# Interleaving the moving columns of a kernel's products, and reading the banks with a step of two

## The chip, the cores and the metric

One core of a Trainium2 chip runs the kernel. The metric is the device time of one execution in microseconds (us). Times and profile come from runs on the chip; the profile is that of one execution. In it PE is TensorE's matrix multiply, PEld its weight load, DVE is VectorE, ACT is ScalarE, POOL is GpSimd, SP issues DMAs.

## The reference

A transformer layer on 1024 rows of width 1024 in float32: a feed-forward block, a token mixer of two parallel groups (sparse attention with three branches, and a gated linear recurrence), a second feed-forward block, and a last norm.

```python
def swiglu(x, w_gu, w_down):
    gate, up = jnp.split(x @ w_gu, 2, axis=-1)
    return (jax.nn.silu(gate) * up) @ w_down

def hybrid_mixer(h, w_in, ...):
    parts = jnp.split(h @ w_in, IN_SPLITS, axis=-1)
    nq, k_c, v_c, k_s, v_s, k_w, v_w, gl, hq, hf, hi, hg = parts
    o_nsa = nsa_group(nq, k_c, v_c, k_s, v_s, k_w, v_w, gl, ...)
    o_hg = hgrn2_group(hq, hf, hi, hg, lower_bound, hg_norm)
    return jnp.concatenate([o_nsa, o_hg], axis=-1) @ w_out

h = h + 0.5 * swiglu(rms_norm(h, ffn1_norm[l]), ffn1_w_gu[l], ffn1_w_down[l])
h = h + hybrid_mixer(rms_norm(h, mix_norm[l]), w_in[l], ...)
h = h + 0.5 * swiglu(rms_norm(h, ffn2_norm[l]), ffn2_w_gu[l], ffn2_w_down[l])
return rms_norm(h, final_norm)
```

The hidden width of the feed-forward blocks is 2752.

## The kernel before

Each float32 operand of a large product is split into two parts that TensorE takes in its fast four-byte format: a rounded high part and the rest (`split`, line 152: ScalarE or GpSimd make the high part in line 157 or 155, VectorE the rest in line 159). A product is then three matrix multiplies into one accumulating bank: high by high, high by low, low by high (`mm3`, lines 161 to 165). A multiply loads a stationary operand of 128 columns and streams a moving operand of up to 512 columns past it. Its output fills a PSUM bank, 128 partitions by 512 float32, one bank column for each moving column.

The stages in order of time:

- The up projection of the first block (to about 470 us): the hidden width is cut into tiles `j` of 128 gate and 128 up columns. Most tiles are computed by `up_strassen` (line 645), a scheme with 7 block products in place of 8, of four `mm3` each. The moving operand is `xT`, 512 columns of the transposed input; the stationary one a piece `wp` of the weights. Three banks P, Q and T take the sums; VectorE adds them up (lines 659, 662, 671, 676, 680) and ScalarE copies one (line 656). `up_out` (line 519) applies the gate and writes the hidden tile `hk` out. `up_plain` and `up_last` do the first tiles and the last, narrow one.
- The down projection (`down`, line 685; to about 700 us): seven stages by the same scheme, 11 steps each; `products` (lines 715 to 717) streams 512 columns of the split weights `dw`. `copies` (line 702) and `add` (line 696) read the banks.
- The mixer (to about 1310 us): projections of queries, keys, values, gates (`gemm_fm`, `gemm_fm_steps` with moving `xT`, `gemm_tm_steps` in lines 780 to 782 with moving weights of 280 or 256 columns, `hgrn_values` and `wout`); the recurrence (`hgrn_unit`) with many small products; attention (`att_soft`, `att_pv`), where scores are products of lines 1219 and 1220, weights are transposed in line 1305, split in lines 1307 and 1308, and multiplied with the values in line 1296 with 512 moving columns (four heads by 128 queries).
- The second block, as the first (to the end).

In all of these the moving operand's columns are read from left to right, and what reads a bank (ScalarE and VectorE instructions) reads its columns from left to right as well. The banks come from pools of a few buffers, so a product into a reused bank waits until what reads it is done. Instructions of an engine run in the order in which they were issued; the pools and a few `late` and `ordered` sections set it.

Some moving reads are by nature of other shapes and aren't touched: scores (up to 512 columns of the keys), transposes, the recurrence's products of 32 to 128 columns, the compression's of 126. VectorE has reads with a step in line 931 (every second value of a tile, twice) and in line 1029 (through a view of `cr` in which neighbouring values lie 16 apart, 64 bytes).

Of the kernel before, what the change touches and what calls it, by code (L numbers as in the profile page):

```python
# [41 lines left out]

def offsets(spec):
    at, o = {}, 0
    for k, cols in spec.items():
        n = sum(b - a for a, b in cols)
        at[k] = o, n
        o += n * D
    return at


def tiled(w, spec):

# [19 lines left out]
class Net:  # L73
# [87 lines left out]
    def mm3(self, ps, wh, wl, xh, xl, first, last, skip=False):  # L161
        mm = self.nc.tensor.matmul
        mm(ps, wh, xh, start=first, stop=False, skip_group_check=skip)  # L163
        mm(ps, wh, xl, start=False, stop=False, skip_group_check=skip)  # L164
        mm(ps, wl, xh, start=False, stop=last, skip_group_check=skip)  # L165
# [353 lines left out]
    def up_out(self, H, j, half, g, u, R, n=128, dve=False):  # L519
# [51 lines left out]
    def up_plain(self, P, groups, js, ws, R, H):  # L571
# [3 lines left out]
        V = {}  # L575
        for ks in groups:
# [3 lines left out]
            for kts in ((0, 1), (2, 3)) if ks[0][2] else ((0,), (1,), (2, 3)):  # L580
                for j, e, o in ks:
# [4 lines left out]
                    if o == 0 and 3 in kts:  # L586
                        nc.scalar.activation(out=P[j, e], in_=V[j, e][:], func=AF.Copy)
            yield
        for j in js:
            self.up_out(H, j, 0, V[j, 0], V[j, 1], R, dve=True)  # L590
# [10 lines left out]
            for k, b in zip(ks, W):  # L601
                nc.vector.tensor_tensor(out=P[k], in0=b[:], in1=P[k], op=OP.add)
            self.up_out(H, j, 1, P[j, 0], P[j, 1], R, dve=True)
# [23 lines left out]
    def up_last(self, wpool, cpool, j, raw, R, H):  # L627
# [6 lines left out]
        nc.scalar.activation(out=p[:], in_=V[:], func=AF.Copy)  # L634
# [3 lines left out]
        u = ct("pu")  # L638
        nc.vector.tensor_copy(out=u[:64], in_=V[64:])
        self.up_out(H, j, 0, V, u, R, 64, True)  # L640
        nc.vector.tensor_tensor(out=p[:], in0=Wb[:], in1=p[:], op=OP.add)
        u = ct("pu")
        nc.vector.tensor_copy(out=u[:64], in_=p[64:])
        self.up_out(H, j, 1, p, u, R, 64, True)

    def up_strassen(self, cpool, j, w, nxt, R, H, sums):
# [7 lines left out]
        p, c12, c22 = ct("pp"), ct("pc"), ct("pd")  # L654
        self.up_mm(P[:], w[0], 0, True, True)
        nc.scalar.activation(out=p[:], in_=P[:], func=AF.Copy)
        step()
        self.up_mm(Q[:], w[1], 4, True, True)
        tt(out=c12[:], in0=Q[:], in1=p[:], op=OP.add)
        step()  # L660
        self.up_mm(T[:], w[2], 3, True, True)
        tt(out=c22[:], in0=T[:], in1=p[:], op=OP.add)
# [8 lines left out]
        tt(out=c22[:], in0=Q[:], in1=c22[:], op=OP.add)  # L671
# [4 lines left out]
        tt(out=c12[:], in0=T[:], in1=c12[:], op=OP.add)  # L676
# [3 lines left out]
        tt(out=p[:], in0=Q[:], in1=p[:], op=OP.add)  # L680
        step()
        self.up_out(H, j, 0, P, p, R, dve=True)
        return out

    def down(self, pool, pool2, name, H, h, scale, final, after=(), wide=None, tail=0):
# [7 lines left out]
        def add(half, t, c, src):  # L693
            tt = half * 4 + t
            hv = h[tt][:, c * 512:c * 512 + 512]
            nc.vector.scalar_tensor_tensor(out=hv, in0=src[:], scalar=scale(tt), in1=hv, op0=OP.mult, op1=OP.add)

        def copies(bs, tag):
            p = H["pool"] if tag == "hk" else pool2
            out = [p.tile([128, 512], F32, name=self.nm(tag), tag=tag, bufs=4) for _ in range(4)]  # L700
            for t in range(4):
                nc.scalar.activation(out=out[t][:], in_=bs[t][:], func=AF.Copy)
            return out
# [3 lines left out]
        for n, (an, bn) in enumerate(stages):  # L707
# [4 lines left out]
            def products(t, m, hh, hl, dh, dl):  # L712
                c = slice(t * 128, t * 128 + 128)
# [43 lines left out]
            for t in range(4):  # L757
                for a in left:
                    products(t, *a)
                if n in (1, 4, 5, 6):  # L760
                    half, c = {1: (1, 0), 4: (0, 0), 5: (0, 1), 6: (1, 1)}[n]
                    add(half, t, c, bs[t])
# [69 lines left out]
    def hgrn_proj(self, p, wp, x, hh, u, w=None):  # L832
# [3 lines left out]
        for half in range(2):  # L836
# [4 lines left out]
            nc.scalar.activation(out=q[:], in_=b[:], func=AF.Sigmoid)  # L841
            nc.vector.tensor_tensor(out=q[:], in0=b[:], in1=q[:], op=OP.mult)
# [4 lines left out]
            nc.scalar.activation(out=f[:], in_=b[:], func=AF.Sigmoid)  # L847
            nc.scalar.activation(out=k[:], in_=b[:], func=AF.Sigmoid, scale=-1.0)
# [4 lines left out]
    def hgrn_gate(self, wp, x, hh, u):  # L853
# [3 lines left out]
        for half in range(2):  # L857
# [3 lines left out]
            nc.scalar.activation(out=g[:], in_=b[:], func=AF.Sigmoid)  # L861
            nc.vector.tensor_tensor(out=g[:], in0=b[:], in1=g[:], op=OP.mult)

    def hgrn_values(self, p, wp, x, vs):
# [13 lines left out]
        for half in range(2):  # L878
            bs = [self.bank() for _ in range(4)]
            for kt in range(KT):  # L880
                for t, b in enumerate(bs):
                    c = slice(t * 128, t * 128 + 128)
                    self.mm3(b[:], x[0][kt // 2][half][:, kt % 2, c], x[1][kt // 2][half][:, kt % 2, c], *w[kt], kt == 0, kt == KT - 1)
                    if kt == KT - 1:
                        v = p.tile([128, 512], F32, name=self.nm("v"), tag="vg", bufs=8)
                        nc.scalar.activation(out=v[:], in_=b[:], func=AF.Copy)
# [103 lines left out]
    def compress_in(self, mop, w, x, raw):  # L990
# [3 lines left out]
        for half in range(2):  # L994
            for s, r in enumerate(raw):
                b = self.bank()
                self.gemm_fm(b[:], w, s * 128, 128, x, half)
                nc.scalar.activation(out=r[:, half * 512:half * 512 + 512], in_=b[:], func=AF.Copy)
# [92 lines left out]
    def att_proj_kv(self, p, wp, x):  # L1091
# [15 lines left out]
        for s in range(2):  # L1107
            for half in range(2):
# [3 lines left out]
                nc.scalar.activation(out=r[:], in_=b[:], func=AF.Copy)  # L1112
                self.kraw[s][half] = r

    def att_proj_q(self, p, wp, x, half, tag, tiles=range(4)):

        nc = self.nc
        for i in tiles:
# [8 lines left out]
            for e in range(2):  # L1127
# [3 lines left out]
                hi = t[g * 64:g * 64 + 64, :]  # L1131
                lo = t[64 - g * 64:128 - g * 64, :]
                src = b[e * 64:e * 64 + 64, :]
# [146 lines left out]
    def att_pv(self, p, g, qb, Ps, raw, M):  # L1280
# [12 lines left out]
        def pv(n):  # L1293
            i, c, w, v = blocks[n]
            for k, t in enumerate((th, tl)):
                mm(O[:], v, t[n][:w], start=n + k == 0, stop=n == last and k == 1)  # L1296
# [20 lines left out]
        nc.scalar.activation(out=tmp, in_=O[64:128].rearrange("p (h q) -> p h q", h=4), func=AF.Copy)  # L1317
        qc = slice((qb % 4) * 128, (qb % 4) * 128 + 128)
        r = p.tile([128, 4, 128], F32, name=self.nm("os"), tag="pt", bufs=5)[:, :2] if M else raw[:, :, qc]
        for e in range(2):  # L1320
            nc.vector.tensor_tensor(out=r[e * 64:e * 64 + 64], in0=O[0:64].rearrange("p (h q) -> p h q", h=4)[:, e::2, :],
                                    in1=tmp[:, e::2, :], op=OP.add)
# [4 lines left out]
    def wout(self, p, M, half, hspill):  # L1327
# [3 lines left out]
        for cq in range(4):  # L1331
            c = slice(cq * 256, cq * 256 + 256)
            w = self.wpages(cq, self.wq_tile)
            for tt in range(half * 4, half * 4 + 4):
# [6 lines left out]
                nc.vector.tensor_tensor(out=r[:], in0=b[:, :256], in1=r[:], op=OP.add)  # L1341
# [3 lines left out]
def body(ctx, tc, ins, out):  # L1345
# [355 lines left out]
    for c in range(2):  # L1701
# [35 lines left out]
        for i in range(4):  # L1737
            hv = h[i][:, c * 512:c * 512 + 512]
            nc.vector.tensor_tensor(out=hv, in0=bs[i][:], in1=hv, op=OP.add)
# [106 lines left out]
```

## Time and profile before

| what | value |
| --- | --- |
| time, median of 3 runs | 1974.97 us |
| lowest, highest | 1974.3, 1979.25 us |
| span of the profiled execution | 1975.0 us |
| mean granted TensorE clock | 0.999 |
| instructions | 31355 |
| matrix multiplies | 11054 |
| DMA | 304.31 MB, mean 154 GB/s |

The span is that from the first to the last instruction of the profiled execution; it is within 0.03 us of the median, so the time of that execution is its span as far as the runs can tell. A row of the groups gives line, engine, operation, output and input names, shapes and count, then the busy time in us and the mean ns of one, then the idle time before it and what ended it. A row of the timeline gives the start and the length in us. Matrix multiplies are pipelined: the recorded length of one reaches into the next, so that the distance of two starts, and not the length, is what a product costs in a row of products.

### The profile page before, as it was taken

How to read it: one execution, taken by the hardware profiler on the slowest of the kernel's cores; microseconds unless marked ns; L12 is line 12 of the kernel's file. 1: busy time of each engine (PE TensorE's matmuls, PEld its weight loads, DVE VectorE, ACT ScalarE, POOL GpSimd, SP SyncE). 2: the span in 40 equal slices, each digit the busy share in tenths (PEclk: the TensorE clock that was granted, in tenths of full speed). 3: DMA queues.
4: the chain of work that ended last, by engine and by line, in shares of the span. 5: the costliest groups of instructions: out<-in, count | busy, mean ns of one | idle time of the engine just before them, and what ended most of it. 6: DMA issues, size and time to landing. Idle time of an engine off the chain costs nothing.

```text
span 1975.0 us, 31355 instructions
## 1 busy us (share of the span) xinstructions
PE 1954.0 (99%) x11054; PEld 1617.0 (82%) x11054; DVE 1380.0 (70%) x2811; ACT 790.3 (40%) x1665; POOL 500.3 (25%) x612
## 2 busy tenths in 40 slices
PE   9999999999999999999999999999999999999998
PEld 6888888888888888879887888788888888888886
DVE  5987778758765635777378888747767777558677
ACT  5532333312323313333379767645333333323233
POOL 2132233323431001011056543211121222123221
PEclk9999999999999999999999999999999999999999
DMA  5346666438774232333311022362446665157563
GB/s 192 110 131 202 218 201 222 142 113 281 236 241 137 80 100 87 136 135 123 125 65 44 26 85 86 117 240 80 165 170 209 215 211 192 65 208 238 185 213 137
DMA packets 161789, 304.31 MB, mean 154 GB/s; under 512 B 17600, under 2 KB 47328, under 8 KB 161632
## 3 DMA queue, kind: packets, MB, share of 16 engines
q1 hardware_dynamic: 152096, 285.79, 42.9%
q10 hardware_dynamic: 9536, 16.53, 2.4%
q8 instruction: 87, 1.43, 0.3%
q14 instruction: 70, 0.57, 0.1%
HBM read 213.65 MB, written 88.60 MB: 153 GB/s over the span
## 4 chain that ended last, share of the span: by engine, by line
PE 91%; DVE 3%; ACT 2%; DMA 1%; issue 1%; POOL 1%; SPq 0%; DVEq 0%; ACTq 0%; POOLq 0%
PE b L163 18%; PE b L165 18%; PE b L164 18%; PE b L715 7%; PE b L717 7%; PE b L716 7%; PE b L1296 3%; PE b L1305 3%; PE b L1220 1%; PE b L1219 1%; PE b L780 1%; PE b L909 1%; PE b L781 1%; PE b L782 1%; ACT P L1262 1%
## 5 line engine op out<-in xcount | busy, mean ns | idle before, releaser
L164 PE MATMUL b<-xT,wp 128*128 128x512 f32 x1196 | 466.4, 390 | 1.4 <-DVE xT L411 1.3
L163 PE MATMUL b<-xT,wp 128*128 128x512 f32 x1196 | 466.4, 390 | 0.7 <-DVE pd L671 0.6
L165 PE MATMUL b<-xT,wp 128*128 128x512 f32 x1196 | 465.9, 390 | 0.4 <-DVE wp L159 0.4
L159 DVE TENSOR_TENSOR dw<-dr,dw 128x512 fp32r<-128x512 f32 x308 | 235.0, 811 | 73.1 <-ACT dw L157 59.5
L163 PEld LDWEIGHTS b<-xT,wp 128*128 128x128 f32 x1196 | 224.5, 188 | 50.5 <-issue 1.7
L164 PEld LDWEIGHTS b<-xT,wp 128*128 128x128 f32 x1196 | 224.6, 188 | 49.1 <-DVE xT L411 2.7
L165 PEld LDWEIGHTS b<-xT,wp 128*128 128x128 f32 x1196 | 224.6, 188 | 47.3 <-DVE wp L159 0.8
L715 PE MATMUL b<-dw,dw 128*128 128x512 f32 x616 | 240.3, 390 | 0.8 <-DVE dw L159 0.8
L717 PE MATMUL b<-dw,dw 128*128 128x512 f32 x616 | 240.2, 390 | 0.2 <-DVE dw L159 0.2
L716 PE MATMUL b<-dw,dw 128*128 128x512 f32 x616 | 240.0, 390 | 0.0
L157 ACT ACTIVATE wp<-ws 128x512 fp32r<-128x512 f32 x148 | 93.3, 632 | 253.0 <-PE b L164 239.0
L155 POOL TENSOR_SCALAR dw<-dr 128x512 fp32r<-128x512 f32 x154 | 121.5, 795 | 275.2 <-PE b L717 158.1
L157 ACT ACTIVATE dw<-dr 128x512 fp32r<-128x512 f32 x154 | 92.4, 627 | 202.3 <-PE b L715 106.5
L1274 POOL TENSOR_SCALAR P<-P,sm,gate 128x64 f32<-128x64 f32 (+8 forms) x192 | 127.2, 679 | 175.4 <-DVE sm L1265 107.8
L159 DVE TENSOR_TENSOR wp<-ws,wp 128x512 fp32r<-128x512 f32 x148 | 110.5, 749 | 41.3 <-ACT wp L157 41.2
L715 PEld LDWEIGHTS b<-dw,dw 128*128 128x128 f32 x616 | 115.7, 188 | 25.2 <-issue 1.5
L717 PEld LDWEIGHTS b<-dw,dw 128*128 128x128 f32 x616 | 115.7, 188 | 24.8 <-DVE dw L159 0.9
L716 PEld LDWEIGHTS b<-dw,dw 128*128 128x128 f32 x616 | 115.7, 188 | 23.9
L157 ACT ACTIVATE wp<-wr 128x512 fp32r<-128x512 f32 x115 | 72.2, 629 | 155.1 <-PE b L164 135.9
L163 PE MATMUL b<-xT,wh 128*128 128x512 f32 x320 | 129.9, 407 | 0.0
L1262 ACT ACTIVATE P<-P,sm 128x64 f32<-128x64 f32 (+8 forms) x192 | 114.8, 600 | 28.4 <-DVE sm L1225 27.9
L165 PE MATMUL b<-xT,wl 128*128 128x512 f32 x320 | 125.5, 392 | 0.0
(316 smaller groups left out, 3520.0 us busy)
## 6 DMA issues: line engine op xcount, KB each, us to landing
dr<-hs SPq DMA_DIRECT2D x242, 256.0 KB, 3.8
wr<-in_ffn_w_gu_dram SPq DMA_DIRECT2D x82, 512.0 KB, 4.1
hs<-hk SPq DMA_DIRECT2D x140, 256.0 KB, 3.7
hs<-wd SPq DMA_DIRECT2D x88, 256.0 KB, 3.0
wd<-in_ffn_w_down_dram SPq DMA_DIRECT2D x84, 256.0 KB, 3.3
dr<-in_ffn_w_down_dram SPq DMA_DIRECT2D x62, 256.0 KB, 4.4
wq<-wo SPq DMA_DIRECT2D x40, 256.0 KB, 3.0
wo<-wo SPq DMA_DIRECT2D x16, 512.0 KB, 2.6
```

Of the source, the lines that this page charges most:

```text
L155: nc.gpsimd.tensor_scalar(out=hi, in0=src, scalar1=1.0, scalar2=1.0, op0=OP.mult, op1=OP.mult)
L157: nc.scalar.activation(out=hi, in_=src, func=AF.Copy)
L159: eng.tensor_tensor(out=lo, in0=src, in1=hi.bitcast(F32), op=OP.subtract)
L163: mm(ps, wh, xh, start=first, stop=False, skip_group_check=skip)
L164: mm(ps, wh, xl, start=False, stop=False, skip_group_check=skip)
L165: mm(ps, wl, xh, start=False, stop=last, skip_group_check=skip)
L715: mm(bs[t][:], hl[:, c], dh, start=first, stop=False, skip_group_check=True)
L716: mm(bs[t][:], hh[:, c], dh, start=False, stop=False, skip_group_check=True)
L717: mm(bs[t][:], hh[:, c], dl, start=False, stop=last, skip_group_check=True)
L1262: nc.scalar.activation(out=rng[br], in_=rng[br], func=AF.Exp, scale=-1.0, bias=m, accum_out=st[:, 6 + br:7 + br])
L1274: nc.gpsimd.tensor_scalar(out=rng[br], in0=rng[br], scalar1=st[:, 6 + br:7 + br], scalar2=self.gate[:, qb, h * 3 + br:h * 3 + br + 1], op0 ...
L1296: mm(O[:], v, t[n][:w], start=n + k == 0, stop=n == last and k == 1)
```

## The change

The moving operand of the large products is read in another order: its columns are taken in turn from the left and the right half, 0, 256, 1, 257 and so on (`il`). The bank still fills from left to right, so it holds the columns in that order. What reads a bank takes every second column of it, first the even ones and then the odd ones (`ev`), and writes them as two halves (`nat`), so that tiles in memory keep their old order. In the value product of attention the halves are those of each head's 128 queries (64 and 64). For the projection with 280 columns the host lays the weights out so that the bank comes out in the old order, and its readers stay as they are. In the output projection (256 columns) the halves are 128 wide.

Not changed: the scores, the transposes, the recurrence's and the compression's products, the count of instructions, and their order on each engine, which is the same instruction by instruction with the same tiles. The changed multiplies of 512 columns have a moving operand of 256 pairs with a distance of 256 values within a pair.

```diff
+def il(x, d=None):
+    if d is None:
+        return x.rearrange("p (a b) -> p b a", a=2)
+    return x.rearrange("p (t a b) -> p t b a", a=2, b=d)
+
+def ev(b, d=None):
+    if d is None:
+        return b.rearrange("p (b a) -> p a b", a=2)
+    return b.rearrange("p (t b a) -> p t a b", a=2, b=d)
+
+def nat(x, d=None):
+    if d is None:
+        return x.rearrange("p (a b) -> p a b", a=2)
+    return x.rearrange("p (t a b) -> p t a b", a=2, b=d)
...
         t = np.concatenate([w[:, a:b] for a, b in cols], axis=1)
+        if t.shape[1] == 280:
+            t = t.reshape(D, 140, 2).transpose(0, 2, 1)
...
     def mm3(self, ps, wh, wl, xh, xl, first, last, skip=False):
-        mm = self.nc.tensor.matmul
+        mm, xh, xl = self.nc.tensor.matmul, il(xh), il(xl)
...
-        src = g[:n]
+        sn, src = nat(s[:n]), g[:n]
         if R is not None:
-            e.tensor_tensor(out=s[:n], in0=src, in1=R[:n], op=OP.mult)
-            src = s[:n]
-        nc.scalar.activation(out=s[:n], in_=src, func=AF.Silu)
-        e.tensor_tensor(out=s[:n], in0=s[:n], in1=u[:n], op=OP.mult)
+            e.tensor_tensor(out=sn, in0=src, in1=nat(R[:n]), op=OP.mult)
+            src = sn
+        nc.scalar.activation(out=sn, in_=src, func=AF.Silu)
+        e.tensor_tensor(out=sn, in0=sn, in1=u[:n], op=OP.mult)
...
-        p, c12, c22 = ct("pp"), ct("pc"), ct("pd")
+        p, c12, c22 = (nat(ct(n)[:]) for n in ("pp", "pc", "pd"))
+        p_, q_, t_ = (ev(b[:]) for b in (P, Q, T))
         self.up_mm(P[:], w[0], 0, True, True)
-        nc.scalar.activation(out=p[:], in_=P[:], func=AF.Copy)
+        nc.scalar.activation(out=p, in_=p_, func=AF.Copy)
         step()
         self.up_mm(Q[:], w[1], 4, True, True)
-        tt(out=c12[:], in0=Q[:], in1=p[:], op=OP.add)
+        tt(out=c12, in0=q_, in1=p, op=OP.add)
...
-            nc.vector.scalar_tensor_tensor(out=hv, in0=src[:], scalar=scale(tt), in1=hv, op0=OP.mult, op1=OP.add)
+            nc.vector.scalar_tensor_tensor(out=nat(hv), in0=src, scalar=scale(tt), in1=nat(hv), op0=OP.mult, op1=OP.add)
...
-                c = slice(t * 128, t * 128 + 128)
+                c, dh, dl = slice(t * 128, t * 128 + 128), il(dh), il(dl)
...
-            wh, wl = w[0][kt][:, :n], w[1][kt][:, :n]
+            wh, wl = il(w[0][kt][:, :n]), il(w[1][kt][:, :n])
...
-                mm(O[:], v, t[n][:w], start=n + k == 0, stop=n == last and k == 1)
+                mm(O[:], v, il(t[n][:w], 64), start=n + k == 0, stop=n == last and k == 1)
...
-                nc.vector.tensor_tensor(out=r[:], in0=b[:, :256], in1=r[:], op=OP.add)
+                nc.vector.tensor_tensor(out=nat(r[:]), in0=ev(b[:, :256]), in1=nat(r[:]), op=OP.add)
```

The same two rewrites (`ev` on a bank, `nat` on the tile it goes to) stand at every other reader of these banks: the copies and adds of `up_plain`, `up_last` and `copies`, the projections of the recurrence, the keys and the queries, and the sums of attention.

More of the change, by code (lines that the diff above doesn't have):

```diff
@@ L601, in up_plain @@
             for k, b in zip(ks, W):
-                nc.vector.tensor_tensor(out=P[k], in0=b[:], in1=P[k], op=OP.add)
-            self.up_out(H, j, 1, P[j, 0], P[j, 1], R, dve=True)
+                nc.vector.tensor_tensor(out=nat(P[k]), in0=ev(b[:]), in1=nat(P[k]), op=OP.add)
+            self.up_out(H, j, 1, nat(P[j, 0]), nat(P[j, 1]), R, dve=True)
             yield
@@ L633, in up_last @@
         self.up_mm(V[:], w[0], 0, True, True)
-        nc.scalar.activation(out=p[:], in_=V[:], func=AF.Copy)
+        pn = nat(p[:])
+        nc.scalar.activation(out=pn, in_=ev(V[:]), func=AF.Copy)
         self.up_mm(Wb[:], w[0], 3, True, False)
@@ L637, in up_last @@
         self.up_mm(Wb[:], w[1], 2, False, True)
[L638 to L644, printed above, removed]
+        u = nat(ct("pu")[:])
+        nc.vector.tensor_copy(out=u[:64], in_=ev(V[64:]))
+        self.up_out(H, j, 0, ev(V[:]), u, R, 64, True)
+        nc.vector.tensor_tensor(out=pn, in0=ev(Wb[:]), in1=pn, op=OP.add)
+        u = nat(ct("pu")[:])
+        nc.vector.tensor_copy(out=u[:64], in_=pn[64:])
+        self.up_out(H, j, 1, pn, u, R, 64, True)
     def up_strassen(self, cpool, j, w, nxt, R, H, sums):
@@ L670, in up_strassen @@
         self.up_mm(Q[:], w[4], 5, False, True)
-        tt(out=c22[:], in0=Q[:], in1=c22[:], op=OP.add)
+        tt(out=c22, in0=q_, in1=c22, op=OP.add)
         step()
@@ L675, in up_strassen @@
         self.up_mm(T[:], w[5], 2, False, True)
-        tt(out=c12[:], in0=T[:], in1=c12[:], op=OP.add)
+        tt(out=c12, in0=t_, in1=c12, op=OP.add)
         step()
@@ L679, in up_strassen @@
         self.up_mm(Q[:], w[6], 6, False, True)
-        tt(out=p[:], in0=Q[:], in1=p[:], op=OP.add)
+        tt(out=p, in0=q_, in1=p, op=OP.add)
         step()
-        self.up_out(H, j, 0, P, p, R, dve=True)
+        self.up_out(H, j, 0, p_, p, R, dve=True)
         return out
@@ L701, in copies @@
             for t in range(4):
-                nc.scalar.activation(out=out[t][:], in_=bs[t][:], func=AF.Copy)
-            return out
+                nc.scalar.activation(out=nat(out[t][:]), in_=ev(bs[t][:]), func=AF.Copy)
+            return [nat(t[:]) for t in out]
         stages = (("A11", "B11"), ("A12", "B21"), ("S2", "T2"), ("S3", "T3"), ("A22", "T4"), ("S1", "T1"), ("S4", "B22"))
@@ L761, in down @@
                     half, c = {1: (1, 0), 4: (0, 0), 5: (0, 1), 6: (1, 1)}[n]
-                    add(half, t, c, bs[t])
+                    add(half, t, c, ev(bs[t][:]))
                     if n == 6:
@@ L997, in compress_in @@
                 self.gemm_fm(b[:], w, s * 128, 128, x, half)
-                nc.scalar.activation(out=r[:, half * 512:half * 512 + 512], in_=b[:], func=AF.Copy)
+                nc.scalar.activation(out=nat(r[:, half * 512:half * 512 + 512]), in_=ev(b[:]), func=AF.Copy)
             yield
@@ L1320, in att_pv @@
         for e in range(2):
-            nc.vector.tensor_tensor(out=r[e * 64:e * 64 + 64], in0=O[0:64].rearrange("p (h q) -> p h q", h=4)[:, e::2, :],
-                                    in1=tmp[:, e::2, :], op=OP.add)
+            nc.vector.tensor_tensor(out=r[e * 64:e * 64 + 64].rearrange("p h (a b) -> p h a b", a=2), in0=ev(O[0:64], 64)[:, e::2],
+                                    in1=tmp[:, e::2, :].rearrange("p h (a b) -> p h a b", a=2), op=OP.add)
         if M:
@@ L1738, in body @@
             hv = h[i][:, c * 512:c * 512 + 512]
-            nc.vector.tensor_tensor(out=hv, in0=bs[i][:], in1=hv, op=OP.add)
+            nc.vector.tensor_tensor(out=nat(hv), in0=ev(bs[i][:]), in1=nat(hv), op=OP.add)
             net.square(np_, hv, sq[:, c, i:i + 1])
```

30 lines of the change are left out of this document (15 added, 15 removed).

## Prediction

> **What bounds the kernel.** I read the page's head first, then its 40 slices, then the chain that ended last, then who TensorE waited for.
>
> ```profile
> span 1975.0 us, 31355 instructions
> ...
> PE 1954.0 (99%) x11054; PEld 1617.0 (82%) x11054; DVE 1380.0 (70%) x2811; ACT 790.3 (40%) x1665; POOL 500.3 (25%) x612
> ...
> PE   9999999999999999999999999999999999999998
> ...
> DVE  5987778758765635777378888747767777558677
> ...
> PEclk9999999999999999999999999999999999999999
> ...
> PE 91%; DVE 3%; ACT 2%; DMA 1%; issue 1%; POOL 1%; SPq 0%; DVEq 0%; ACTq 0%; POOLq 0%
> ```
>
> TensorE is busy in every slice, at its full granted clock, and carries 91% of the chain. The view of TensorE's waits is short; its longest entry is
>
> ```profile
> PE b L1296 <- ACT ph L1307: 2.2, 4, 0.7
> ```
>
> so there is hardly a wait to win: the kernel's time is the number of products times the spacing of their starts. A page's "mean ns of one" does not give that spacing, since one product's record overlaps the next (390 ns in the groups below). The spacing comes from the timeline of TensorE alone: the first and the last row of 61 products in a row in the first down projection (512 columns), of 17 in the output projection (256), and of 23 in the value projection (280).
>
> ```profile
> 582.84 0.39 PE L715 MATMUL b<-dw,dw 128*128 128x512 f32 x1
> ...
> 596.44 0.39 PE L715 MATMUL b<-dw,dw 128*128 128x512 f32 x1
> ```
>
> ```profile
> 1270.39 0.28 PE L781 MATMUL b<-wq,xT 128*128 128x256 f32 x1
> ...
> 1272.29 0.28 PE L782 MATMUL b<-wq,xT 128*128 128x256 f32 x1
> ```
>
> ```profile
> 912.99 0.29 PE L781 MATMUL b<-wl,xT 128*128 128x280 f32 x1
> ...
> 915.83 0.29 PE L782 MATMUL b<-wh,xT 128*128 128x280 f32 x1
> ```
>
> 13.60 us over 60 steps is 226.7 ns; 1.90 over 16 is 118.8 ns; 2.84 over 22 is 129.1 ns. From 256 to 512 columns 107.9 ns are added, 0.421 ns for each column; from 280 to 512 it is 97.6 ns, again 0.421. So 512 columns take 215.5 ns and **about 11 ns of each product do not depend on the columns**. That is all there is to win in the order of the columns, unless a column can go through in less than 0.421 ns, for which no row speaks.
>
> **What the change touches.** Nothing is added, removed or moved: on each of the five engines the same instructions stand in the same order, with the same tiles; only the steps inside an operand differ. The touched products, one row for each group of three lines (of the three lines 163 to 165, 715 to 717 and 780 to 782, each has the same count), and the two lists of line 1296, each there twice (ph and pt):
>
> ```profile
> L163 PE MATMUL b<-xT,wp 128*128 128x512 f32 x1196 | 466.4, 390 | 0.7 <-DVE pd L671 0.6
> L715 PE MATMUL b<-dw,dw 128*128 128x512 f32 x616 | 240.3, 390 | 0.8 <-DVE dw L159 0.8
> L163 PE MATMUL b<-xT,wh 128*128 128x512 f32 x320 | 129.9, 407 | 0.0
> L1296 PE MATMUL b<-ph,vhl 128*128 128x512 f32 x132 | 59.1, 448 | 2.4 <-ACT ph L1307 1.9
> L780 PE MATMUL b<-wq,xT 128*128 128x256 f32 x128 | 36.4, 284 | 0.0
> L163 PE MATMUL b<-wh,xT 128*128 128x512 f32 x64 | 26.2, 409 | 0.0
> L780 PE MATMUL b<-wh,xT 128*128 128x280 f32 x64 | 19.5, 305 | 0.0
> L163 PE MATMUL b<-wp,xT 128*128 128x512 f32 x48 | 19.2, 399 | 0.0
> L163 PE MATMUL b<-xT,wx 128*128 128x512 f32 x32 | 13.0, 406 | 0.0
> L1296 PE MATMUL b<-ph,vcm 128*128 128x512 f32 x16 | 7.2, 448 | 0.3 <-ACT ph L1307 0.3
> L163 PE MATMUL b<-wq,xT 128*128 128x512 f32 x16 | 6.2, 389 | 0.0
> ```
>
> With 512 columns: 3 x (1196 + 616 + 320 + 64 + 48 + 32 + 16) + 2 x (132 + 16) = 7172. With 256: 384. With 280: 192. Together 7748 of 11054, and 7172 x 0.2267 + 384 x 0.1188 + 192 x 0.1291 = 1696 us, 86% of the span. Scores, transposes and the recurrence's small products are left as they are.
>
> **Term 1: the moving read.** No row of before has a moving operand with a step, so this is bounded from both sides. On the good side stands the fixed 11 ns: 7748 x 11 = 85 us. What could it be? Beside each product a weight load runs, always of 128 columns, whatever the product's width:
>
> ```profile
> L715 PEld LDWEIGHTS b<-dw,dw 128*128 128x128 f32 x616 | 115.7, 188 | 25.2 <-issue 1.5
> ```
>
> 188 ns of load under 226.7 ns of product: the load itself is covered, and both fetch 4-byte values from the same memory. A fixed number of fetches that hold the stream up for a moment gives a fixed term like the 11 ns; a stream that alternates between two places may let them in between. That is a reading, and no row proves it. On the bad side stand VectorE's rows, the only ones with steps in a read:
>
> ```profile
> L1341 DVE TENSOR_TENSOR res<-b,res x16: 418/421/425, 1111.5 to 1273.5; 128x256 f32<-128x256 f32 x16
> ```
>
> ```profile
> L931 DVE TENSOR_TENSOR ft<-f x8: 416/420/424, 693.0 to 891.4; 128x256 f32<-128x256 f32 x8
> ```
>
> ```profile
> L1029 DVE TENSOR_TENSOR fl<-cr,posT x16: 1007/1019/1036, 682.6 to 722.9; 64x504 f32<-64x504 f32 x16
> ```
>
> ```profile
> L659 DVE TENSOR_TENSOR pc<-b,pp 128x512 f32<-128x512 f32 x37 | 25.5, 690 | 20.8 <-PE b L165 20.8
> ```
>
> ```profile
> L656 ACT ACTIVATE pp<-b 128x512 f32<-128x512 f32 x37 | 21.5, 581 | 0.3 <-PE b L165 0.3
> ```
>
> L931 reads every second value of both its inputs (256 of 512) and takes 420 ns, as the plain add of 256 values in line 1341 does: a step of 8 bytes costs nothing. L1029 reads its first input with a step of 64 bytes and takes 1019 ns for 504 values where L659 takes 690 for 512: about 0.66 ns more for each value. Carried over to TensorE, that would be 0.66 x 512 = 338 ns a product. So the ends are -85 us and, at 7172 x 338 ns, +2.4 ms.
>
> The Trainium skill has a rule against this change: "SBUF — State Buffer", Door 1, says that the memory is read in 16-byte lines and that a line needs two or more hits for full bandwidth, with a penalty for each crossing to another line. The two VectorE rows agree with it (8-byte steps 420 ns, 64-byte steps 1019 ns). Here each column would cross to another line, though each line is come back to after one column; by the rule's letter the change loses, and the rival below carries that.
>
> Another part of the Trainium skill speaks for a removable fixed part: "TensorE: Matmul & The Clock Gate", Part 1, puts a warm product's start-to-start at N / 2.4 GHz plus some 2.5 ns, 215.8 ns for 512 columns, where this trace has 226.7. By that rule 10.9 ns of each product are not the array's own; the sum from it would be 84 us, the same as from the rows.
>
> I take nearly the whole fixed part as gone, since a stream slowed at all would be slowed by far more than 11 ns, and the alternation either leaves room for the loads or does not. In the attention stage I take half, as there other engines set part of the pace:
>
> ```profile
> 1000.00:1150.00 150.00, 146.20 (x873) 120.73 (x872) 129.15 (x443) 120.36 (x333) 81.51 (x132) 1.00 0.16 50
> 1150.00:1310.00 160.00, 157.27 (x973) 133.29 (x972) 112.02 (x313) 100.43 (x218) 47.71 (x60) 1.00 0.37 120
> ```
>
> (PE, PEld, DVE, ACT, POOL busy with their counts.) VectorE is at 86% and ScalarE at 80% in the first of these. The 1846 products there, touched or not, could bring 20 us at 11 ns; I leave out 10 us. Term 1: -85 + 10 = **-75 us**.
>
> **Term 2: the evacuations.** What reads a bank now takes every second column, both halves one after the other; the writes stay in runs of 256. Between nothing (L931's case, 8 bytes) and 0.66 ns a value (L1029's case), so 0 to 338 ns for 512 values, and below nothing is excluded, since L659's 690 ns already is that of a plain contiguous add. I take 0, the nearest row being the 8-byte one. The cover if it isn't: the up projections have 84 products a tile, 84 x 226.7 = 19.0 us, and VectorE in the stretch below is at 81%:
>
> ```profile
> 60.00:360.00 300.00, 299.44 (x1321) 247.65 (x1320) 242.53 (x386) 101.84 (x172) 87.58 (x66) 1.00 0.57 191
> ```
>
> Six reads of banks a tile (five adds and the output's) at 0.338 us are 2.0 us beside 15.4 of 19.0. With the products at 216 ns a tile takes 18.1 us, and 17.4 us of VectorE still fit.
>
> **Sum.** 1975.0 - 75 + 0 = **1900 us**. The profiled span, 1975.0, is the median of the shown runs (1974.97) to 0.03 us, so nothing has to be added around it.
>
> **The rivals.**
> (a) *The fixed part has nothing to do with the read* (a change of weights, say): for it, it is the same whatever the columns; against it, nothing in the rows. Then nothing moves: 1975, from 1970 to 1980.
> (b) *The stream is slower.* Place: each touched product; mechanism: a column that isn't in the line just read waits for a second fetch. If a column takes twice its 0.421 ns, a 512-column product takes 215.5 ns more, and 7172 x 215.5 + 384 x 107.8 + 192 x 118 ns = 1610 us: 3585 us. It decides early: from 11 / 512 = 0.02 ns a column the gain is gone. For it: L1029. Against it: each line is used four times within eight columns, and L931 shows that two uses a line suffice on VectorE.
> (c) *The products are unchanged or a little better, and the evacuations are slower.* 0.338 us on each read of a bank puts VectorE at 92% in the up projections; its queue is in order, and behind a late add stand the splits (line 159) that TensorE's weights come from. If a tenth of the added 2.0 us of a tile came through, 37 tiles would lose 7 us, and the last adds at the end about 1 us: 1975 to 1995. It decides from 0.6 us more a read, where 15.4 + 6 x 0.6 reach 19.0.
>
> **How the numbers follow.** Forecast 0.54, own range 1880 to 1935 (from 95 us, where the 11 ns are 12.3 by the timeline's steps of 0.01 us, to 42 us, half the fixed part); (a) 0.13; (c) 0.13; (b) 0.20. The range takes in the forecast, (a) and (c), and leaves (b) out: 1878 to 1995. A measurement of this kernel can tell some 0.3%, 6 us, from no change: faster 0.54, same 0.13, slower 0.33.
>
> **What would show it.** The spacing over 60 products of a down projection: 216 to 218 ns where the forecast holds, 226.7 for (a) and (c), 400 or more for (b). The 256-column spacing tells whether the loss or gain goes with the columns (b) or with the product (forecast). L659 at 690 ns and L656 at 581 show term 2 right; 1000 ns and more show (c). The forecast is wrong if the products' spacing does not move, or if it does and VectorE's splits then are late: the wait on line 159 in the group of line 715, 0.8 us now, would grow to tens.

## Result and profile after

| | before | after |
| --- | --- | --- |
| median of 4 runs | 1975.07 us | 1910.07 us |
| lowest, highest | 1974.3, 1979.25 us | 1908.56, 1911.33 us |
| span of the profiled execution | 1975.0 us | 1909.6 us |

The ratio is 0.9669, 95% interval 0.9656 to 0.9683: 65.0 us less, where 75 were forecast. The span of an execution runs from its first to its last instruction and is shorter than its time: the profiled execution of the kernel after took 1911.33 us with a span of 1909.6, and 13 executions of the kernel before, taken with a later experiment, each had a span some 1.7 us below their time. So the span of 1975.0 us before, equal to the median time, seems to belong to an execution of some 1976.7 us; the difference of the spans below is good to a us or two. Of the 31361 instructions after, 6 more than before, the added ones are semaphore instructions (five on TensorE, one on VectorE); the counts of all that is shown as busy are the same. Below are the head of the page of the kernel after, its slices (of TensorE, VectorE and the clock) and the chain's shares.

```profile
span 1909.6 us, 31361 instructions
...
PE 1875.9 (98%) x11054; PEld 1621.0 (85%) x11054; DVE 1379.4 (72%) x2811; ACT 788.2 (41%) x1665; POOL 511.4 (27%) x612
...
PE   9999999999999999999999999999999999999997
...
DVE  5988878757766635777378888847877777558677
...
PEclk9999999999999999999999999999999999999999
...
PE 82%; DVE 9%; ACT 4%; issue 2%; DMA 2%; POOL 1%; SPq 0%; ACTq 0%; DVEq 0%; POOLq 0%
```

TensorE's busy time fell by 78.1 us (1954.0 to 1875.9), the span by 65.4, VectorE's busy time not at all (1380.0 to 1379.4). TensorE still carries most of the chain, but VectorE's share has grown from 3% to 9%: the products are faster, and now here and there something is late for them, as the waits further down show.

The timeline of TensorE after, first and last row of 61 products of 512 columns in the same down projection, and of 20 of 280 columns in the value projection:

```profile
519.64 0.38 PE L741 MATMUL b<-dw,dw 128*128 128x512 f32 x1
...
532.59 0.38 PE L741 MATMUL b<-dw,dw 128*128 128x512 f32 x1
```

```profile
884.08 0.28 PE L806 MATMUL b<-wl,xT 128*128 128x280 f32 x1
...
886.34 0.28 PE L807 MATMUL b<-wh,xT 128*128 128x280 f32 x1
```

12.95 us over 60 steps is 215.8 ns, 10.9 less than before; 2.26 over 19 is 118.9 ns, 10.2 less. Per product the gain is about the same for 280 columns as for 512, so it goes with the product, not with the column. The groups of the bank's readers after (`L684` was line 659, `L681` was 656):

```profile
L684 DVE TENSOR_TENSOR pc<-b,pp 128x512 f32<-128x512 f32 x37 | 25.4, 687 | 14.8 <-PE b L188 14.8
...
L681 ACT ACTIVATE pp<-b 128x512 f32<-128x512 f32 x37 | 21.4, 580 | 0.0
```

687 ns where it was 690, and 580 where it was 581: a read of every second column of a bank costs these two nothing. TensorE's waits after, the longest sums first (line waiting, what for: us in total, times, longest):

```profile
PE b L1321 <- ACT ph L1332: 3.7, 8, 0.9
PE b L186 <- DVE pd L696: 3.5, 3, 1.7
PE b L934 <- DVE q L943: 3.4, 4, 1.6
PE b L740 <- DVE dw L182: 3.0, 3, 1.1
PE b L742 <- DVE dw L182: 2.5, 1, 2.5
```

Two rows of the same view of before go with them (line 909 is `L934` after, line 717 is `L742`):

```profile
PE b L909 <- DVE q L918: 1.6, 2, 1.3
PE b L717 <- DVE dw L159: 0.2, 1, 0.2
```

The longest sum was 2.2 us; now there are four of 3 us and more, and waits on VectorE's split (`L182`, before line 159) reach 2.5 us at one time.

The matrix multiplies stand in one order in both kernels, so the k-th start can be compared with the k-th. Summed by stage of the time before (touched products times 10.9 ns, against what the stage really became shorter by):

| stage (us of before) | touched x 10.9 ns | saved | left over |
| --- | --- | --- | --- |
| 0 to 470, up projection | 21.7 | 19.0 | 2.7 |
| 470 to 560, first part of the down projection | 4.3 | -1.3 | 5.6 |
| 560 to 800, its rest and the first projections | 9.8 | 10.2 | -0.4 |
| 800 to 1000, projections and recurrence | 8.2 | 4.8 | 3.4 |
| 1000 to 1310, attention and output | 9.4 | 3.4 | 6.0 |
| 1310 to the end, second block | 31.1 | 29.4 | 1.7 |
| sum (of unrounded rows) | 84.5 | 65.4 | 19.1 |

Each row rests on one execution of each kernel. In the profiles of two other kernels with plain products (experiments 4 and 7 below) the stage from 800 to 1000 us is 1.8 and 1.9 us shorter than in this kernel before and the first one 0.5 and 1.0, the others differ by 0.2 at most. So the first and the fourth left-over are good to 1 or 2 us only; the stage from 470 to 560 took 90.0 us in all three.

So two things had to be explained: what the 10.9 ns are, and where some 19 us of them went. The stage from 470 to 560 even lost. The timeline of TensorE there, in the kernel after (in brackets the idle time before it, and its releaser):

```profile
486.51 0.45 PE L740 MATMUL b<-dw,dw 128*128 128x512 f32 x1 [1.07 <-DVE dw L182]
486.80 0.38 PE L741 MATMUL b<-dw,dw 128*128 128x512 f32 x1
489.65 0.79 PE L742 MATMUL b<-dw,dw 128*128 128x512 f32 x1 [2.47 <-DVE dw L182]
490.24 0.63 PE L740 MATMUL b<-dw,dw 128*128 128x512 f32 x1
490.66 0.63 PE L741 MATMUL b<-dw,dw 128*128 128x512 f32 x1
```

and of VectorE:

```profile
484.73 0.61 DVE L182 TENSOR_TENSOR wl<-wr,wh 128x256 fp32r<-128x256 f32 x1
485.27 1.09 DVE L182 TENSOR_TENSOR dw<-dr,dw 128x512 fp32r<-128x512 f32 x1
486.29 2.71 DVE L721 SCALAR_TENSOR_TENSOR h<-b,hr,h 128x512 f32<-128x512 f32 x4
488.92 0.67 DVE L182 TENSOR_TENSOR dw<-dr,dw 128x512 fp32r<-128x512 f32 x1
```

A product waits for the low part of its weights (`dw`), whose subtraction stands on VectorE's queue behind four adds of 2.71 us and behind pieces of another weight's split (`wl`, the mixer's `c` weights, placed between the steps of this stage). After the gap the products come 0.42 to 0.43 us apart, twice the normal spacing. The windows show why (us, busy of PE, PEld, DVE, ACT, POOL with counts, granted clock, DMA share, GB/s):

```profile
482.70:486.00 3.30, 2.74 (x13) 2.07 (x11) 3.30 (x5) 0.00 (x0) 3.30 (x6) 1.00 0.68 249
486.00:489.50 3.50, 0.67 (x2) 0.30 (x2) 3.50 (x6) 2.38 (x7) 0.63 (x1) 1.00 0.58 182
489.50:492.90 3.40, 3.25 (x8) 2.62 (x9) 2.67 (x6) 1.44 (x4) 0.30 (x1) 0.51 0.90 274
```

The granted clock is 0.51 in the 3.4 us behind a stretch in which TensorE did two products. The loss is thus the gaps of 1.07 and 2.47 us, and then half of 3.4 us once more: about 5.2 us of the 5.6. GpSimd, which makes some of the high parts, is busy without a break in the first window too (3.30 of 3.30 us); but VectorE never waits there or in the second, so it is its own queue that is late.

### The profile page after: what moved, and what is told of

It reads as the page before. It is cut to its first block, busy times and chain, and to the rows that moved or that the text cites. A ratio compares the mean times of both kernels' runs of the same rounds, so it can differ in the third digit from the quotient of the medians.

```text
span 1909.6 us, 31361 instructions
## 1 busy us (share of the span) xinstructions
PE 1875.9 (98%) x11054; PEld 1621.0 (85%) x11054; DVE 1379.4 (72%) x2811; ACT 788.2 (41%) x1665; POOL 511.4 (27%) x612
## 4 chain that ended last, share of the span: by engine, by line
PE 82%; DVE 9%; ACT 4%; issue 2%; DMA 2%; POOL 1%; SPq 0%; ACTq 0%; DVEq 0%; POOLq 0%
PE b L186 17%; PE b L188 17%; PE b L187 17%; PE b L742 6%; PE b L740 6%; PE b L741 6%; PE b L1330 2%; PE b L1321 2%; ACT P L1287 1%; ACT ph L1332 1%; PE b L1245 1%; PE b L1244 1%; PE b L934 1%; DVE dw L182 1%; PE b L805 1%
## 5 line engine op out<-in xcount | busy, mean ns | idle before, releaser
L186 PE MATMUL b<-xT,wp 128*128 128x512 f32 x1196 | 453.9, 380 | 4.0 <-DVE pd L696 3.5
L187 PE MATMUL b<-xT,wp 128*128 128x512 f32 x1196 | 453.7, 379 | 1.6 <-DVE xT L434 1.5
L188 PE MATMUL b<-xT,wp 128*128 128x512 f32 x1196 | 453.2, 379 | 0.0
L182 DVE TENSOR_TENSOR dw<-dr,dw 128x512 fp32r<-128x512 f32 x308 | 230.7, 796 | 69.7 <-ACT dw L180 48.8
L186 PEld LDWEIGHTS b<-xT,wp 128*128 128x128 f32 x1196 | 226.0, 189 | 40.4 <-DVE pd L696 4.7
L740 PE MATMUL b<-dw,dw 128*128 128x512 f32 x616 | 234.7, 381 | 3.1 <-DVE dw L182 3.0
L742 PE MATMUL b<-dw,dw 128*128 128x512 f32 x616 | 234.8, 381 | 2.5 <-DVE dw L182 2.5
L741 PE MATMUL b<-dw,dw 128*128 128x512 f32 x616 | 234.0, 380 | 0.0
L178 POOL TENSOR_SCALAR dw<-dr 128x512 fp32r<-128x512 f32 x154 | 128.9, 844 | 256.9 <-PE b L742 131.0
L182 DVE TENSOR_TENSOR wp<-ws,wp 128x512 fp32r<-128x512 f32 x148 | 114.4, 775 | 30.3 <-ACT wp L180 30.1
L742 PEld LDWEIGHTS b<-dw,dw 128*128 128x128 f32 x616 | 116.8, 190 | 20.3 <-DVE dw L182 3.8
L186 PE MATMUL b<-xT,wh 128*128 128x512 f32 x320 | 126.5, 396 | 0.0
L530 POOL TENSOR_TENSOR ws<-wr 128x512 f32<-128x512 f32 x37 | 51.7, 1398 | 272.5 <-DVE wp L182 223.7
```

Source lines behind the costliest of these rows:

```text
L178: nc.gpsimd.tensor_scalar(out=hi, in0=src, scalar1=1.0, scalar2=1.0, op0=OP.mult, op1=OP.mult)
L182: eng.tensor_tensor(out=lo, in0=src, in1=hi.bitcast(F32), op=OP.subtract)
L530: nc.gpsimd.tensor_tensor(out=s3[:], in0=a11, in1=a21, op=OP.subtract)
L740: mm(bs[t][:], hl[:, c], dh, start=first, stop=False, skip_group_check=True)
L741: mm(bs[t][:], hh[:, c], dh, start=False, stop=False, skip_group_check=True)
L742: mm(bs[t][:], hh[:, c], dl, start=False, stop=last, skip_group_check=True)
```

## The experiments

The letters are those of the expectations. A line is 16 bytes of memory, four 4-byte values, as in the prediction. For the 10.9 ns: **A**, the weight load's reads hold up the stream, so the loss goes with the number of loaded columns; **B**, a plain read loses a fixed time for each product, whatever its width; **C**, it loses a little for each line, so with the columns. For the time not gained: **D**, the crowded VectorE queue of the first down projection.

**1. Orders of the columns.** A kernel in which the layer is left out: rows of 48 products, 128 loaded columns, 512 moving ones, one row for each order of the moving columns.

```diff
+    segments = [
...
+        lambda b, s, e: mm(b, w, x, start=s, stop=e),
+        lambda b, s, e: mm(b, w, il(x), start=s, stop=e),
+        lambda b, s, e: mm(b, w, blocks(x, 64), start=s, stop=e),
...
+        lambda b, s, e: mm(b, w, every(x, 2), start=s, stop=e),
...
+    for f in segments:
+        for t in range(4):
+            for k in range(12):
+                f(bs[t][:], k == 0, k == 11)
```

> A kernel of its own that leaves the layer out: 24 rows of 48 products each, back to back, accumulating in four banks, each row with another read of the moving or the stationary operand (512 moving columns, 128 loaded ones, four-byte values, where nothing else is said). Read is the distance of the starts within a row. All theories: plain 226.7 ns, interleaved halves 215.8 ns, as in the two traces. Theory A (the weight load's fetches hold the plain stream up): the excess over the interleaved row goes with the fetches of the load: with 64 loaded columns about 221 ns, with 32 about 218 ns; with loaded columns that lie 2 or 4 values apart (twice and four times as many 16-byte lines) 230 to 260 ns; interleaved 216 ns whatever is loaded. Theory B (a fixed cost of changing weights or of starting a plain stream): plain stays at 226.7 ns with 64 or 32 loaded columns and with loads that lie apart. On the order: if alternation alone does it, pairs 4, 8 or 64 columns apart give 216 ns as halves do; if it takes two far places, blocks of 4 and 8 stay near 226.7. If the line rule held for TensorE, reads with a step of 4 or 16 values, a new 16-byte line for each column, would take 400 ns and more; if any order but the plain one is fast, these take 216 ns too. bf16 plain: 216 ns if the excess belongs to four-byte operands, 226.7 if to every load.

The timeline of TensorE in this kernel; the distance from one row's start to the next, by 48, is the spacing:

```profile
30.02 10.52 PE L52 MATMUL b<-xt,wt 128*128 128x512 f32 x48
40.38 10.52 PE L53 MATMUL b<-xt,wt 128*128 128x512 f32 x48
50.74 10.52 PE L54 MATMUL b<-xt,wt 128*128 128x512 f32 x48
61.10 10.52 PE L55 MATMUL b<-xt,wt 128*128 128x512 f32 x48
71.46 11.10 PE L56 MATMUL b<-xt,wt 128*128 128x512 f32 x48
82.39 16.48 PE L57 MATMUL b<-xt,wt 128*128 128x512 f32 x48
98.69 12.18 PE L58 MATMUL b<-xt,wt 128*128 128x512 f32 x48
110.71 21.82 PE L59 MATMUL b<-xt,wt 128*128 128x512 f32 x48
132.34 22.32 PE L60 MATMUL b<-xt,wt 128*128 128x512 f32 x48
154.49 20.98 PE L61 MATMUL b<-xt,wt 128*128 128x512 f32 x48
175.29 13.77 PE L62 MATMUL b<-xt,wt 128*128 128x512 f32 x48
188.90 23.58 PE L63 MATMUL b<-xt,wt 128*128 128x512 f32 x48
212.29 11.54 PE L64 MATMUL b<-xt,wt 128*128 128x512 f32 x48
223.67 11.36 PE L65 MATMUL b<-xt 128*128 128x512 f32 x48
```

| line | order of the 512 columns | ns a product |
| --- | --- | --- |
| L52 | two halves in turn (0, 256, 1, 257, ...) | 215.8 |
| L53, L54, L55 | pairs 64, 8, 4 apart | 215.8 |
| L56 | pairs 2 apart (0, 2, 1, 3, ...) | 227.7 |
| L57 | two halves, two columns at a time (0, 1, 256, 257, ...) | 339.6 |
| L58 | two halves, four columns at a time | 250.4 |
| L59, L60, L61 | every 2nd, 4th, 16th column, pass after pass | 450.6, 461.5, 433.3 |
| L62, L63 | four, eight places in turn | 283.5, 487.3 |
| L64 | plain, begun one value later | 237.1 |

(L59: 132.34 - 110.71 = 21.63 us, by 48.) The plain order's row (L51) stands first of the four-byte ones, and its beginning is slower (20 products in the 4.77 us from 18.90); the timeline from 23.67 us on has its last 28 products, up to the start of L52 at 30.02:

```profile
23.67 6.51 PE L51 MATMUL b<-xt,wt 128*128 128x512 f32 x28
```

(30.02 - 23.67) / 28 is 226.8 ns, as in the kernel before. The gain of the kernel comes back with nothing but the order, and it doesn't need halves: pairs 4 values apart, 16 bytes, do as well (pairs 64 apart are also how the value product of attention reads), and pairs inside 16 bytes do nothing. The other orders in the table are slower than the plain one, by some 24 ns and more; only the plain one begun one value later loses less (10 ns). In the same run a plain read with 64 and 32 loaded columns took 230 and 232 ns (268.59 - 257.55 and 279.71 - 268.59 us, by 48), not less than with 128: theory A in its simple form fell.

**2. What the fixed part depends on.** The same with 24 products in halves ahead of rows of 96, and other widths, loads and types.

```diff
+        lambda b, s, e, k: mm(b, w, x, start=s, stop=e),
+        lambda b, s, e, k: mm(b[:, :448], w, x[:, :448], start=s, stop=e),
+        lambda b, s, e, k: mm(b[:, :448], w, il(x[:, :448]), start=s, stop=e),
...
+        lambda b, s, e, k: mm(b[:32], w[:, :32], x, start=s, stop=e),
...
+        lambda b, s, e, k: mm(b, w, x, start=True, stop=True),
...
+        lambda b, s, e, k: mm(b, wb[:], il(xb[:]), start=s, stop=e),
```

> A kernel of its own that leaves the layer out: rows of 96 products, each behind 24 interleaved ones so that all start from the same state; read is the distance of the starts in the second half of a row. The first series refuted theory A in its simple form (64 or 32 loaded columns did not bring the plain row down) but its rows were disturbed by the ones before. Theory A (the load's fetches meet the stream's): plain with 64 and 32 loaded columns below 226.7; loads that lie 2 or 4 values apart cost more, and with interleaved columns too. Theory B (a fixed cost at a plain stream's start or end): plain keeps 13 ns over its columns at 0.417 ns each for 448, 384 and 320 columns (200, 173, 147 ns), for any load, for 64 rows in place of 128, for one bank or without accumulation; interleaved keeps 2.5 ns (189, 162.5, 136). Theory C (a cost for each line of the plain stream): the excess falls with the columns, to 7 ns at 320. Alternating plain and interleaved products: 221 ns on average if each pays for itself, 216 or 227 if one rules the other. bf16: 216 ns plain (seen); interleaved the same if the limit is the four-byte stream, 300 ns and more with a step of two if the line rule holds there too.

From its timeline: the rows of 384 columns, plain (L55) and in halves (L56), with the 24 products between (L50), and further down the 16-bit type in halves.

```profile
87.45 16.83 PE L55 MATMUL b<-xt,wt 128*128 128x384 f32 x96
104.12 5.34 PE L50 MATMUL b<-xt,wt 128*128 128x512 f32 x24
109.30 15.76 PE L56 MATMUL b<-xt,wt 128*128 128x384 f32 x96
124.89 5.34 PE L50 MATMUL b<-xt,wt 128*128 128x512 f32 x24
...
606.64 46.68 PE L76 MATMUL b<-xb,wb 128*128 128x512 bf16 x96
652.70 5.80 PE L50 MATMUL b<-xt,wt 128*128 128x512 f32 x24
```

384 columns: 173.6 ns plain (104.12 - 87.45 us by 96), 162.4 in halves (124.89 - 109.30 us by 96). In the same way, over the second half of each row, its last step left out: 226.7 and 215.8 with 512 columns, 202.7 and 189.2 with 448, 146.7 and 135.8 with 320. The difference is 11 to 14 ns at each width: in this **B holds and C falls**, since a loss per line would shrink with the columns. It is also 226.7 without accumulation, into one bank, with 64 rows of weights, and 230.0 and 231.7 with 64 and 32 loaded columns. Plain and halves alternating gave 231.7 and 215.0: each product pays for its own order. The load isn't out of it, though, so the second half of B, the same loss with any load, does not hold: a load that reads every 4th value makes it 235.0 plain and 236.7 in halves, and takes the whole gain back. With the 16-bit type a plain product takes 216.1 ns ((601.26 - 580.95) us by the 94 in the profile), so there is no such loss to win back, and in halves it takes 480 ns (46.06 us by 96). One order in this kernel is a warning: pairs 4 values apart, begun one value later, take 266.8 ns ((521.75 - 496.14) us by 96) where the first experiment had 215.8. Begun there, two values of one line (7 and 4) follow one another in each block of eight (1, 5, 2, 6, 3, 7, 4, 8).

**3. Alignment.** The same, with the moving operand, the pairs' distance and the load moved by some values.

```diff
+        lambda b, s, e, k: mm(b, w, xt[:, 4:516], start=s, stop=e),
+        lambda b, s, e, k: mm(b, w, il(xt[:, 1:513]), start=s, stop=e),
...
+        lambda b, s, e, k: mm(b, w, far(257), start=s, stop=e),
...
+        lambda b, s, e, k: mm(b, xt[:, 514:642], x, start=s, stop=e),
+        lambda b, s, e, k: mm(b, xt[:, 514:642], il(x), start=s, stop=e),
```

> A third kernel of its own that leaves the layer out, built like the second: rows of 96 products behind 24 interleaved ones. It asks where the cost sits. Theory G (the stream is cut into 16-byte lines of four values, and two lines are held at a time): what counts is where the lines are cut. Plain or interleaved starts 4 values on change nothing (226.7 and 215.8); plain starts 1 or 2 values on are slower than 226.7 (1 value on gave 236.7); interleaved starts 1 or 2 values on still 215.8, since two lines are in turn all the same; pairs 257 or 258 apart, where the two lines end at different columns, 215.8 or a little more. If it is the distance within a pair in whole lines that counts, 257 and 258 are slow (over 260, as the shifted blocks of 4 were) and 260 is 215.8. 510 columns: 225.8 plain, 215.0 interleaved, if nothing hangs on whole lines at the end. A load that starts 2 values into a line (33 lines in place of 32): no change in either if loads do not matter, some ns in the plain row if they do. 96 loaded columns: plain between 226.7 and the 230 of 64.

The plain read begun 4 values later, a whole line, took 231.7 ns where I expected no change: there theory G fell. A load begun 2 values into a line made the plain read 230.7, the case that was named for loads that matter. In halves it is 215.8 to 216.7 ns with every start (1, 2, 4 values), every distance (257, 258, 260) and that load. Plain reads range from 226.7 to 237 ns by where operand and load begin; halves don't. What holds a plain read up by those 11 to 21 ns stays open: that moving the load moves it speaks for a clash of the two reads, and that fewer loaded columns don't lower it speaks against a count of the load's reads.

**4. The evacuations alone.** The kernel after with the products read from left to right and the banks still read with a step; the columns of its result stand in another order.

```diff
 def il(x, d=None):
+    return x
```

> The changed kernel with the products reading their moving columns from left to right again, while what reads the banks still takes every second column; it leaves out the interleaving, so columns of the result are in another order. Theory F (the gain is the products' alone and the strided bank reads are free): 1974 to 1976 us, as before. Rival (c) of the prediction, strided bank reads that cost: 1980 us and more, and the same cost is hidden in the changed kernel's time. If the stepped bank reads had a part in the gain: below 1970.

Its time was 1976.98 us (before, on the same chip, 1976.2), ratio 1.0003, interval 0.9994 to 1.0013. The reads with a step cost nothing that this can tell (0.1%, 2 us), and the order of the products is the whole gain.

**5. The down projections back.** The kernel after with `il`, `ev` and `nat` doing nothing in `down`.

```diff
+        il = ev = nat = lambda x: x
```

> The changed kernel with both down projections as before (plain moving columns, plain bank reads). 1848 of the 7748 products get their 10.9 ns back, 20.1 us. Theory D (the stall of the first down projection comes from its own faster products, which leave VectorE no time): the stall goes too, 1910 + 20.1 - 5.3 = 1925 us. If the stall comes from arriving 18 us earlier, with the hidden tiles' transfers still under way, it stays: 1930 us. If the gain is not the products' own but comes of something else in the stage, another sum.

1924.85 us, ratio 0.9741, interval 0.9725 to 0.9757: by the two ratios (0.9741 - 0.9669) 0.0072 of 1975 us, 14.2 us of the gain, are gone (14.8 by the medians). The two down projections have 3 x 616 = 1848 products, 20.1 us at 10.9 ns; less the 5.6 us that the stall had cost, 14.5 us were to go. That fits D. More directly, its stage from 470 to 560 takes 90.0 us, as before. In its profile the gap is gone (windows as above):

```profile
486.00:489.50 3.50, 3.50 (x17) 2.92 (x16) 3.50 (x7) 3.07 (x8) 0.52 (x2) 1.00 0.80 233
489.50:492.90 3.40, 3.40 (x17) 2.82 (x16) 1.99 (x4) 0.84 (x4) 0.62 (x1) 1.00 0.84 241
```

VectorE is full (3.50 of 3.50 us) in that first window in this kernel too, but the slower products don't overtake it.

**6 and 7. The other weight's split, two stages later.** In the kernel after, and the same in the kernel before as a control:

```diff
-        after[2, 1 + i] = lambda i=i: part("c", i)
+        after[4, 1 + i] = lambda i=i: part("c", i)
```

> The changed kernel, with the eight weight splits for the compression's projection taken out of the third stage of the first down projection and put into its fifth. Theory D (these splits, with the faster products, make VectorE late there, TensorE then waits 3.5 us and loses as much again at half the clock): 4 to 5 us faster than the changed kernel, 1905 to 1906 us, and no product of that stretch 427 ns apart from the next. Rival E (the late ones are the transfers of the hidden tiles, which come as late whatever VectorE does): 1909 to 1911 us.

> The same move of the eight splits in the kernel before, where TensorE does not wait in that stretch: 1974 to 1976 us, no change, by both theories; a gain of over 2 us would mean that the stretch was a bottleneck already.

After: 1906.56 us, ratio 0.965 to before, interval 0.9634 to 0.9666. Before: 1974.61 against 1975.17, ratio 0.9997, interval 0.9988 to 1.0006. The windows of the former:

```profile
486.00:489.50 3.50, 3.50 (x18) 3.06 (x17) 2.29 (x4) 0.81 (x3) 0.62 (x1) 1.00 0.83 221
489.50:492.90 3.40, 3.40 (x17) 2.98 (x16) 1.84 (x4) 2.19 (x4) 2.28 (x3) 1.00 0.78 213
```

35 products where the kernel after had 10 in the same 6.9 us, and the full clock. The stage from 470 to 560 is 5.3 us shorter than after; the span is only 4.3 us shorter (1905.3), since attention is 1.1 us longer and the rest differs by half a us here and there. By the medians this is 3.5 us below after, a little less than the 4 to 5 expected, and the intervals of the two ratios overlap; but the slowest of its four executions (1908.11 us) is still faster than the fastest of the kernel after (1908.56). D holds: the loss was the place of that split, and the move is worth nothing where the products are slower. This is the fastest of all versions run.

## Why the prediction was right, and where it was off

The measured 1910.07 us lies within the range of 1880 to 1935, 10 us above the forecast. (The wider range's lower end, 1878, should have been 1880, the lower end of the forecast's own.)

*The bound.* Right: the time followed the spacing of the products. 10.9 ns times 7748 is 84.5 us, and if no wait had grown the span would have fallen by about that.

*Term 1, the fixed 11 ns.* The size held almost to the tenth, 215.8 ns where 216 to 218 was named, and "do not depend on the columns" held in the second experiment at four widths. Part of that closeness is luck. From 320 to 512 columns that experiment adds 80.0 ns both plain (146.7 to 226.7) and in halves (135.8 to 215.8), 0.417 ns a column; so the part that does not go with the columns is some 13 ns plain and 2.5 in halves. The prediction read 11 for the 13, from rows of 256 and 280 columns, and took all of it as gone where 2.5 stay: two errors that nearly cancel. The reading that went with it, the load's reads let in between, is not shown: the number of loaded columns doesn't matter, though the load's place and step do. The Trainium skill, "TensorE: Matmul & The Clock Gate", Part 1, has N / 2.4 GHz plus some 2.5 ns; the trace agrees for the reads in turn (215.8, 162.4 and 135.8 ns for 512, 384 and 320 columns, where it gives 215.8, 162.5 and 135.8), not for halves of 256 columns (111.7, where it gives 109.2) and not for the plain ones.

*Term 1, the 256-column products.* Before they took 118.8 ns, in the first experiment 119.8 plain and 111.7 in halves (295.82 - 290.07 and 301.18 - 295.82 us by 48): about 8 ns rather than 11. With 384 of them the difference is 1 us.

*Term 1, what comes back.* **This is the term that was mis-sized**: 10 us were left out, 19 came back. For attention I halved 20 us, but those were 11 ns for all 1846 products of that stage, touched or not; the touched ones hold 9.4 us, of which 6.0 came back, so there the 10 us were too many. Nothing was left out elsewhere, where 13 us came back: 5.6 in the first down projection, of which experiments 5 to 7 show 5.3 with their cause; 3.4 beside the recurrence, where a wait of 1.65 us for line 943 (1.3 before) is likewise followed by half the clock, as these windows of the kernel after show; and some 4 in the up projections and at the end, where the wait of `L186` on `L696` has grown from 0.6 to 3.5 us. For these two and for attention no experiment was made, and their causes stay open. The half clock can be only a part of the 3.4: in the fifth experiment the wait at the same place is 2.3 us, the clock stays whole, and that stage still saves only 5.6 of its 8.2 us.

```profile
779.00:782.40 3.40, 1.41 (x67) 0.93 (x66) 2.56 (x6) 0.81 (x3) 0.00 (x0) 1.00 0.47 154
782.40:786.00 3.60, 3.60 (x26) 2.88 (x14) 2.18 (x7) 0.00 (x0) 0.00 (x0) 0.59 0.48 150
```

The step that missed it was the cover by averages: the prediction took something off only where long stretches show busy engines (attention), and an average over a long stretch says nothing of 3.5 us in which VectorE's queue holds 3.5 us of work. Already in the kernel before VectorE is busy 12.99 of the 13.5 us from 479.4 to 492.9. The sign named in the prediction, the wait on the split, did grow, from 1.0 us (0.8 and 0.2) to 5.5 in lines 740 and 742, not to tens.

*Term 2, the evacuations.* Right at 0: 687 and 580 ns, and the fourth experiment.

*The rivals.* (a) fell with the spacing. (c) fell with term 2. (b) fell here, but it is the rule for nearly all other orders: every second column takes 450.6 ns, more than the doubled 431 that it was priced at. Of the two reasons against it, the second, that two uses of a line suffice on VectorE, does not carry over to TensorE: every second column uses each line twice and is slow. The Trainium skill, "SBUF — State Buffer", Door 1, asks for two hits or more in a 16-byte line; every second column has just two of them one after the other, yet takes 450.6 ns, while the halves leave the line after each value and are the fastest. By these rows the rule as written does not hold for TensorE's moving reads. What the rows of four-byte values have in common is only this: where two lines are read in turn, one value of each, a product of 512 columns takes 215.8 to 216.7 ns, if the load reads no more sparsely than every second value. Why is not shown.

## What to carry to other kernels

Where TensorE is the bound, measure the distance of its starts at two widths before looking for waits: a part that doesn't go with the columns can sit in how the operand is read, and for the four-byte products here two lines in turn took most of it away (11 of 13 ns), at no cost in the banks' readers. Try the very order first in a row of bare products, since neighbouring orders cost up to twice the time. And when the bound engine gets faster by a few per cent, look for the single stretches, not the averages, in which another engine's queue was just in time: moving eight small pieces of work out of such a stretch gave back 5.3 us there.

## What the runs showed of the hardware that was not expected

- The stall of 3.5 us cost nearly half as much again: in the 3.4 us behind it the granted clock was 0.51 and the products came 427 ns apart. In the kernel before this never happened within the run, in the one after twice. The Trainium skill, "TensorE: Matmul & The Clock Gate", Part 1, has the clock go to half after an idle window of about 3.4 us; the trace agrees nearly in the first place, with two products in 3.5 us ahead of the 0.51. In the second TensorE was busy 1.41 of the 3.40 us ahead, with 67 products, 64 of them of 32 columns, so the window was far from idle. The length of the wait alone does not decide either: 1.65 us were followed by half the clock there, and 2.3 us at the same place in the fifth experiment were not.
- Two places in turn take 215.8 ns, four 283.5, eight 487.3; and two values at a time from two places 339.6, four at a time 250.4.
- The same order that gains 11 ns with four-byte values makes a product of two-byte ones take 480 ns, where read plainly it takes 216.
- A load that reads every second value is free beside halves (215.8 ns), one that reads every fourth costs 21 ns more (236.7).
